# All blocks of the first two modulations asked for at once, with other loads moved behind them

## The chip, the cores and the metric

The kernel runs on one core of a Trainium2 chip. The metric is the device time of one execution in microseconds (us), as the median of several runs. Five engines work side by side, each through its own instructions in order: TensorE (PE in the profile, its weight loads PEld), VectorE (DVE), ScalarE (ACT), GpSimd (POOL) and SyncE (SP). SP computes nothing here; its queue holds nearly all requests for data, and each request goes to DMA engines that copy between HBM and SBUF while the engines work on. A few requests stand in ACT's queue, among its arithmetic.

## The reference

Two layers of a diffusion backbone over 256 latent and 256 context tokens of width 1024. Each layer is a SwiGLU half-step, a token mixer and a second half-step, all of them modulated by vectors that are computed from a conditioning vector with a large matrix `ada_w`:

```
mx = split(silu(c) @ ada_w[i] + ada_b[i], 9)       # latent; mh: the same from c_ctx, for the context
h  = modulate(rms_norm(x, g), shift, scale)         # h * (1 + scale) + shift
x  = x + 0.5 * gate * ((silu(h @ w_gate) * (h @ w_up)) @ w_down)     # half-step, inner width 2816
xn, hn = modulated norms of latent and context; ox, oh = mixer(xn, hn)
x  = x + mx[5] * ox;   then the second half-step, for the latent and (in layer 0) the context
```

The first half-step of a stream needs three of the nine modulation vectors: shift (0), scale (1) and gate (2). Everything is float32.

## The kernel before

**Tiles.** Activations are kept transposed, as 8 tiles of 128 features x 256 tokens per stream. Weights come in blocks of 128 x 1024 (512 KB). A float32 product is made of three matmuls: ACT rounds a half-block to `whi` (line 224), DVE computes the rest `wlo` (line 227), and PE multiplies `hh` by `whi`, `hl` by `whi` and `hh` by `wlo`, 8 such triples for one block.

**The front.** `ada_first` computes shift and scale, in 8 steps `t` of 128 features. Each step asks for two half-blocks of 512 KB (`raw<-in_ada_first`, line 218), multiplies them on PE (8 matmuls, `f` or `aux` `<-raw,scpad`), has ACT copy the sums (`sqa`, line 337), adds on PE (`<-selq,sqa`) and ends with two small operations on DVE (`mod`, lines 340 and 341). With those two `norm_h` makes one of the eight tiles `hh`, `hl` (lines 461, 462 and 467). `abreast` multiplies each tile, as soon as it is there, with the gate and up weights of blocks 0 and 1 of the inner width; these four weight blocks sit in a pool of their own (`front`). When `abreast` has been written out, a callback `done` closes that pool.

**The first half-step of the context** (`ffn00c`). The inner width has 22 blocks of 128. Blocks 2, 3, ... each take two products (a gate and an up block, `f<-hh,whi` and so on), then `gated` (lines 512, 513) and a split (255, 256) whose results are kept in `rows` tiles `ah`, `al`. The blocks are in groups, (0, 8), (8, 15) and (15, 22): after each group `down` multiplies its results with the down weights, 8 products, and adds them to x (`residual`, line 472). Room for weight blocks on the way: 5 tiles `raw`.

**Beside the products.** `next(beside)` runs one step of other modulation work after each block and after every second product of `down`: first 16 steps of `ada_rows` (one block of 512 KB and two products on DVE of 128 x 1024 each, `junk`, line 371; modulations 2 and 3), then steps of `more_ada` (two blocks of 512 KB, 4 or 8 matmuls `aux`). `ada_rows` needs `srow`, 1 MB that `ada_vectors` asks for and sends through Silu on ACT (lines 358, 360). The gate has to be complete before the first `down`, so `ffn` takes further steps there if need be.

**Order.** Each engine runs its instructions in the order of a scheduler that works on the order in which the code is written; generators stand side by side in `weave`, each with a rank and a clock, and `yield "rows"` makes one wait for the mark of that name. All requests share 8 completion slots in turn: a request waits until the request eight before it has landed, on whichever queue that was.

Of the kernel before, what the change touches and what calls it, by code (L numbers as in the profile page):

```python
# [21 lines left out]
NF = 22  # L22
# [1802 lines left out]
class Main(Net):  # L1825
    def run(self):
        self.tc.cur_priority -= 2000
        self.setup()
        self.tc.cur_priority += 2000
        with ExitStack() as self.m0s:  # L1830
            Mixer0.shared(self, self.m0s, "left")
            self.spawn(self.contexts(), 0)
            self.spawn(self.latents(), 0)
            self.weave()

    def contexts(self):

        st, fx, first = ExitStack(), ExitStack(), []
        front = self.pool(fx, "front", "left")

        def begin():
            def after(t):
                if t < 2:
                    first.extend(self.fetch(front, self.I["ffn_gu"][0, 2 * t + e], 4) for e in range(2))
            self.load_x(0)
            with ExitStack() as raw:
                self.ada_first(self.pool(raw, "raw", "left"), 8, after)

        def beside(*at):
            self.ada_vectors(self.pool(st, "st", "left"))  # L1850
            yield from self.steps(self.ada_rows(range(2, 4)), *at)
            st.close()
            self.mark("rows")
            yield from self.more_ada(*at)
        self.ffn(0, 0, 0, "right", "ffn00c", 50, begin=begin, raws=5, bufs=4, rows=8, extra=beside, groups=((0, 8), (8, 15), (15, NF)),
                 front=(front, first), done=fx.close)
        yield "ffn00c"
        self.m0c = Mixer0(self, 0, "right", 10)
        self.m0c.chain(10, None)
        yield "endm00"  # L1860
        self.ffn(0, 1, 0, "right", "ffn01c", 60.5, raws=4, bufs=4, rows=6, tanh=True, extra=self.more_ada)
        yield "ffn10c"
        self.m1.context("right", 30)

    def latents(self):

        yield 20.0
        self.load_x(1)
        Mixer0.consts(self)
        yield "rows"  # L1870
        self.ffn(0, 0, 1, "left", "ffn00x", 60, raws=4, bufs=4, rows=6, tanh=True, extra=self.more_ada)
        yield "ffn00x"
        m0x = Mixer0(self, 1, "left", 20)
# [4 lines left out]
        with ExitStack() as st:  # L1878
            self.ada_vectors(self.pool(st, "st", "left"))
            early, rows = self.ada_rows(range(10, 12)), self.ada_rows(range(12, 18))  # L1880
# [30 lines left out]
```

## Time and profile before

| | us |
|---|---|
| time, median of 3 runs | 2132.99 (2126.71 to 2137.01) |
| the profiled execution, its own time | 2136.58 |
| span of the profiled execution | 2134.7 |
| PE busy | 2041.3 (96%) |
| DVE, ACT busy | 1442.4 (68%), 992.2 (46%) |
| DMA | 361 MB, mean 169 GB/s |
| mean granted clock of PE | 0.976 |

The profiled execution is 3.6 us above the median. All places below are given in us from the start of the span. Three places are used as marks: at 53.43 the front's last modulated tile reaches PE, at 153.8 the 16 steps of `ada_rows` are complete, and at 294.4 the last residual of the first half-step of the context ends.

### The profile page before, as it was taken

Reading aid. Unit: us, or ns where it says so; the run is one execution under the profiler, and the core shown is the slowest. Engines: PE = TensorE matmul, PEld = TensorE weight load, DVE = VectorE, ACT = ScalarE, POOL = GpSimd, SP = SyncE. Lnnn points to the kernel's source line nnn. Section 1 sums busy time; section 2 is a strip of 40 time slices with the busy share of each in tenths; the row PEclk is TensorE's granted clock in tenths of the full one; section 3 lists DMA queues with packets and bytes.
Section 4 is the critical chain, followed back from the end, with each engine's and each line's share of the span. In section 5 each row is a group of like instructions: output and inputs, shape, how many; then the busy total and the mean of one; then the engine's idle time right before and its main releaser. Section 6 shows DMA issues by size and latency. Waiting matters only on the chain.

```text
span 2134.7 us, 41784 instructions
## 1 busy us (share of the span) xinstructions
PE 2041.3 (96%) x16120; PEld 1855.8 (87%) x16120; DVE 1442.4 (68%) x3193; ACT 992.2 (46%) x2084; POOL 195.0 (9%) x364
## 2 busy tenths in 40 slices
PE   6999899999999989999998999999999999998999
PEld 4897778899889889988998999988878987888999
DVE  4794467896567889855678966884654485656554
ACT  3443346554435665534455445432232457435553
POOL 0000006601000194010100000000000010000000
PEclk9899999999999999989999999999999999999999
DMA  8678765555244436622356665674554342224554
GB/s 324 203 259 305 252 236 193 154 181 155 80 136 158 140 119 188 172 87 81 127 192 205 217 229 150 212 232 156 209 168 143 91 134 87 75 86 147 184 178 120
DMA packets 131492, 361.04 MB, mean 169 GB/s; under 512 B 30652, under 2 KB 39612, under 8 KB 131037
## 3 DMA queue, kind: packets, MB, share of 16 engines
q1 hardware_dynamic: 129808, 356.58, 51.0%
q8 instruction: 126, 2.06, 0.4%
q10 hardware_dynamic: 1484, 1.80, 0.3%
q14 instruction: 74, 0.60, 0.1%
HBM read 352.82 MB, written 5.51 MB: 168 GB/s over the span
## 4 chain that ended last, share of the span: by engine, by line
PE 75%; DMA 9%; DVE 8%; ACT 3%; issue 3%; POOL 1%; SPq 0%; DVEq 0%; ACTq 0%; POOLq 0%
PE f L175 45%; PE mm L175 19%; PE g L175 6%; DVE wlo L227 3%; DMA raw<-in_ffn_gu 3%; DMA raw<-in_ada_rows 3%; DMA raw<-in_ffn_down 2%; PE q L175 1%; PE aux L175 1%; ACT whi L224 1%; DVE junk L371 1%; PE mm L185 1%; DVE hn L461 1%; DMA srow<-in_c_rows 1%; DVE x L472 0%
## 5 line engine op out<-in xcount | busy, mean ns | idle before, releaser
L224 ACT CAST whi<-raw 128x512 fp32r<-128x512 f32 (+3 forms) x1082 | 625.8, 594 | 760.7 <-PE f L175 378.0
L227 DVE TENSOR_TENSOR wlo<-raw,whi 128x512 fp32r<-128x512 f32 (+3 forms) x1082 | 709.9, 670 | 339.6 <-ACT whi L224 320.8
L175 PE MATMUL f<-hh,whi 128*128 128x256 f32 x1696 | 487.8, 288 | 9.8 <-ACT whi L224 5.1
L175 PE MATMUL f<-hh,wlo 128*128 128x256 f32 x1696 | 487.6, 288 | 5.4 <-DVE wlo L227 5.3
L175 PE MATMUL f<-hl,whi 128*128 128x256 f32 x1696 | 486.7, 287 | 1.8 <-DVE hl L467 1.7
L175 PEld LDWEIGHTS f<-hh,whi 128*128 128x128 f32 x1696 | 328.5, 194 | 23.5 <-ACT whi L224 12.5
L175 PEld LDWEIGHTS f<-hh,wlo 128*128 128x128 f32 x1696 | 328.4, 194 | 13.5 <-DVE wlo L227 9.6
L175 PEld LDWEIGHTS f<-hl,whi 128*128 128x128 f32 x1696 | 328.8, 194 | 4.0 <-DVE hl L467 3.0
L175 PE MATMUL f<-ah,whi 128*128 128x256 f32 (+1 forms) x1040 | 309.9, 298 | 12.2 <-ACT whi L224 6.9
L175 PE MATMUL f<-ah,wlo 128*128 128x256 f32 (+1 forms) x1040 | 308.7, 298 | 5.8 <-DVE wlo L227 5.6
L175 PE MATMUL f<-al,whi 128*128 128x256 f32 (+1 forms) x1040 | 307.5, 296 | 0.1
L175 PEld LDWEIGHTS f<-ah,whi 128*128 128x128 f32 x1040 | 204.1, 196 | 26.2 <-ACT whi L224 13.6
L175 PEld LDWEIGHTS f<-ah,wlo 128*128 128x128 f32 x1040 | 203.9, 196 | 13.3 <-DVE wlo L227 9.3
L175 PEld LDWEIGHTS f<-al,whi 128*128 128x128 f32 x1040 | 204.3, 196 | 3.9 <-issue 0.5
L371 DVE SCALAR_TENSOR_TENSOR junk<-raw,srow 128x1024 int8<-128x1024 f32 x128 | 156.6, 1223 | 75.1 <-DMA raw<-in_ada_rows 72.9
L175 PE MATMUL mm<-whi,hh 128*128 128x256 f32 x368 | 101.2, 294 | 4.9 <-ACT zk L1548 2.8
L175 PE MATMUL mm<-wlo,hh 128*128 128x256 f32 x368 | 104.8, 291 | 1.1 <-DVE wlo L227 0.9
L175 PE MATMUL mm<-whi,hl 128*128 128x256 f32 x368 | 102.3, 287 | 1.0 <-DVE hl L467 1.0
L255 ACT CAST ah<-sg 128x256 fp32r<-128x256 f32 (+1 forms) x134 | 58.3, 435 | 93.0 <-DVE sg L513 78.8
L472 DVE SCALAR_TENSOR_TENSOR x<-f,mod,x 128x256 f32<-128x256 f32 x144 | 63.5, 479 | 34.3 <-PE f L175 33.6
L175 PEld LDWEIGHTS mm<-whi,hh 128*128 128x128 f32 x368 | 67.8, 192 | 10.1 <-ACT zk L1548 3.8
L175 PEld LDWEIGHTS mm<-wlo,hh 128*128 128x128 f32 x368 | 70.9, 193 | 6.3 <-issue 3.1
(480 smaller groups left out, 3538.5 us busy)
## 6 DMA issues: line engine op xcount, KB each, us to landing
raw<-in_ffn_gu SPq DMA_DIRECT2D x268, 512.0 KB, 4.3
raw<-in_ada_rows SPq DMA_DIRECT2D x80, 512.0 KB, 4.3
raw<-in_ffn_down SPq DMA_DIRECT2D x56, 512.0 KB, 3.9
raw<-in_ada SPq DMA_DIRECT2D x48, 512.0 KB, 5.8
raw<-in_ffn_down SPq DMA_DIRECT2D x56, 384.0 KB, 3.2
raw<-in_ev_qkv SPq DMA_DIRECT2D x24, 512.0 KB, 3.8
raw<-in_ev_nat SPq DMA_DIRECT2D x20, 512.0 KB, 4.2
raw<-in_ffn_down SPq DMA_DIRECT2D x32, 320.0 KB, 3.0
```

Source lines behind the costliest of these rows:

```text
L175: self.nc.tensor.matmul(out, lhsT=lhsT, rhs=rhs, start=start, stop=stop, **kw)
L185: self.nc.tensor.transpose(out, src, self.c["ident"][:n, :n])
L224: self.nc.scalar.copy(hi[:, :w], raw[:, :w])
L227: (self.nc.gpsimd if self.cut % P == P - 1 else self.nc.vector).tensor_tensor(lo[:, :w], raw[:, :w], hi[:, :w], op=ALU.subtract)
L255: self.nc.scalar.copy(pair[0], src)
L371: nc.vector.scalar_tensor_tensor(self.junk, raw, 1.0, self.srow[:, s], op0=ALU.mult, op1=ALU.mult, accum_out=self.mod[:, m, t, s:s + 1])
L461: nc.vector.scalar_tensor_tensor(hn, self.x[s][k], scale, r, op0=ALU.mult, op1=ALU.mult)
L472: self.nc.vector.scalar_tensor_tensor(self.x[s][k], pb, self.mod[:, gate, k, s:s + 1], self.x[s][k], op0=ALU.mult, op1=ALU.add)
```

## The change

- `ada_first` gets room for 16 half-blocks rather than 8: all that it ever asks for.
- `Mixer0.shared`, which reserves the first mixer's room (and the pool for its constants), is called in `done`, so that `ada_first`'s blocks can lie where that room is later.
- `ada_vectors` (the 1 MB `srow`) moves from the start of `beside` into `done`.
- `latents` waits for the mark "rows" before it loads the latent stream x1 and the mixer's constants (`Mixer0.consts`: `const` 611 KB, `ev_rows` 112 KB, `ev_conv` 30 KB, `ev_cols` 5 KB, requested on ACT's queue), rather than for 20.0 on the clock of `weave`.
- The groups of the first half-step become (0, 9), (9, 16) and (16, 22), with 9 `rows` tiles.

```diff
         with ExitStack() as self.m0s:
-            Mixer0.shared(self, self.m0s, "left")
             self.spawn(self.contexts(), 0)
             self.spawn(self.latents(), 0)
             self.weave()
...
             self.load_x(0)
             with ExitStack() as raw:
-                self.ada_first(self.pool(raw, "raw", "left"), 8, after)
+                self.ada_first(self.pool(raw, "raw", "left"), 16, after)
+
+        def done():
+            fx.close()
+            Mixer0.shared(self, self.m0s, "left")
+            self.ada_vectors(self.pool(st, "st", "left"))
 
         def beside(*at):
-            self.ada_vectors(self.pool(st, "st", "left"))
             yield from self.steps(self.ada_rows(range(2, 4)), *at)
             st.close()
             self.mark("rows")
             yield from self.more_ada(*at)
-        self.ffn(0, 0, 0, "right", "ffn00c", 50, begin=begin, raws=5, bufs=4, rows=8, extra=beside, groups=((0, 8), (8, 15), (15, NF)),
-                 front=(front, first), done=fx.close)
+        self.ffn(0, 0, 0, "right", "ffn00c", 50, begin=begin, raws=5, bufs=4, rows=9, extra=beside, groups=((0, 9), (9, 16), (16, NF)),
+                 front=(front, first), done=done)
...
     def latents(self):
 
-        yield 20.0
+        yield "rows"
         self.load_x(1)
         Mixer0.consts(self)
-        yield "rows"
         self.ffn(0, 0, 1, "left", "ffn00x", 60, raws=4, bufs=4, rows=6, tanh=True, extra=self.more_ada)
```

A block of 9 k-tiles of down weights is wider than one `raw` tile, so `product` asks for it as 128 x 1024 and 128 x 128 (64 KB), each in a tile of its own.

What SP asks for in a row, from the tenth request of the front on; x_3 is the latent stream x1, raw a block of weights. Before:

```order
L218 DMA raw_219<-in_ada_first 128x1024
L286 DMA x_3_67<-in_xT 128x1024 x2
L218 DMA raw_221<-in_ada_first 128x1024
L218 DMA raw_536<-in_ffn_gu 128x1024
L218 DMA raw_580<-in_ffn_gu 128x1024
L218 DMA raw_622<-in_ada_rows 128x1024
L218 DMA raw_629<-in_ffn_gu 128x1024
L218 DMA raw_668<-in_ffn_gu 128x1024
L218 DMA raw_238<-in_ada_first 128x1024
```

Five more `ada_first` and `srow` follow. Now, from the same place:

```order
L218 DMA raw_256<-in_ada_first 128x1024
L218 DMA raw_258<-in_ada_first 128x1024
L218 DMA raw_513<-in_ffn_gu 128x1024
L218 DMA raw_557<-in_ffn_gu 128x1024
L218 DMA raw_591<-in_ada_rows 128x1024
L218 DMA raw_598<-in_ffn_gu 128x1024
L218 DMA raw_637<-in_ffn_gu 128x1024
L286 DMA x_3_67<-in_xT 128x1024 x2
L358 DMA srow_501<-in_c_rows 128x2048
L218 DMA raw_671<-in_ada_rows 128x1024
```

The two rows at the head are the last of the 16 blocks; seven blocks that stood ahead of the last six of them (two of x1, four of ffn_gu, one of ada_rows) stand behind now.

ACT near the end of the front, now (before, the four requests stand at the very start of its queue). hh is a modulated tile, sqa the copy of a step's sums, const and the ev_ tiles the first mixer's constants:

```order
L462 ACTIVATE hh_76_323<-hn_322,mod_79 128x256
L292 DMA const_390_1882<-in_const 128x1222
L296 DMA ev_conv_1884<-in_ev_conv 128x60
L296 DMA ev_rows_1886<-in_ev_rows 128x224
L337 COPY sqa_250<-aux_241 128x256
L296 DMA ev_cols_1888<-in_ev_cols 128x10
L462 ACTIVATE hh_79_329<-hn_328,mod_79 128x256
L337 COPY sqa_269<-f_260 128x256
```

The four requests stand ahead of the copies of the last two steps; by the slots in turn they wait for the landing of the last `ada_first` block, of the next two `ffn_gu` blocks and of the `ada_rows` block.

DVE at the end of the front, before: mod is the modulation of one step (L340, L341) or of a row (L371).

```order
L467 SCALAR_TENSOR_TENSOR hl_108_387<-hn_385,mod_79,hh_107_386 128x256
L371 SCALAR_TENSOR_TENSOR junk_618,mod_79<-raw_622,srow_617 128x1024 x2
L340 TENSOR_SCALAR mod_79<-f_280,adab_72 128x2
L341 TENSOR_SCALAR mod_79<-f_280,b_36_133,ng_74 128x2
L461 SCALAR_TENSOR_TENSOR hn_391<-x_2_66,mod_79,q_296 128x256
```

Now the front runs through to its last tile, and the first products with `srow` come 21 instructions after that; the place where they stand now (acc is the sum of squares of x1):

```order
L434 TENSOR_TENSOR acc_5_69<-acc_5_69,sq_386_1872 128x256
L227 TENSOR_TENSOR wlo_656<-raw_637,whi_655 128x512
L513 TENSOR_TENSOR sg_151_632<-sg_151_632,f_510 128x256
L434 TENSOR_TENSOR acc_5_69<-acc_5_69,sq_387_1875 128x256
L256 TENSOR_TENSOR al_512<-sg_151_632,ah_511 128x256
L371 SCALAR_TENSOR_TENSOR junk_502,mod_79<-raw_591,srow_501 128x1024 x2
L227 TENSOR_TENSOR wlo_681<-raw_678,whi_680 128x512
```

What moved: the first two of the 32 products with `srow` from ahead of the last `mod` of the front to behind blocks 2 and 3, and five sums of x1 into that stretch.

## Rows read from the trace of the kernel before

**Rows 1.** The profile's page: PE in 40 slices of 53.4 us; the longest chain.

```profile
PE   6999899999999989999998999999999999998999
PE 75%; DMA 9%; DVE 8%; ACT 3%; issue 3%; POOL 1%; SPq 0%; DVEq 0%; ACTq 0%; POOLq 0%
```

**Rows 2.** Stretches: length, busy time of five engines, PE clock, DMA share, GB/s.

```profile
10.00:46.00 36.00, 30.34 (x227) 19.68 (x227) 16.49 (x50) 12.63 (x29) 0.00 (x0) 0.95 1.02 407
46.00:53.00 7.00, 3.97 (x36) 3.23 (x34) 4.48 (x11) 2.90 (x5) 0.00 (x0) 0.89 0.06 15
53.00:69.00 16.00, 14.45 (x67) 14.16 (x68) 8.46 (x19) 5.85 (x12) 0.00 (x0) 0.51 0.50 157
69.00:92.00 23.00, 23.00 (x194) 23.00 (x193) 20.80 (x44) 11.99 (x25) 0.00 (x0) 1.00 0.60 204
92.00:106.00 14.00, 10.95 (x84) 10.13 (x83) 11.93 (x24) 4.99 (x11) 0.00 (x0) 1.00 0.75 243
106.00:154.00 48.00, 48.00 (x383) 47.03 (x383) 45.06 (x83) 21.09 (x38) 0.00 (x0) 0.96 0.80 261
154.00:294.00 140.00, 127.52 (x940) 104.20 (x941) 66.86 (x138) 54.16 (x110) 0.00 (x0) 0.98 0.76 267
```

**Rows 3.** SP's queue in the front: start, length of the issuing, what.

```profile
17.55 1.61 SPq L286 DMA_DIRECT2D x<-in_xT  x2
...
23.95 0.33 SPq L218 DMA_DIRECT2D raw<-in_ada_rows  x1
25.22 1.62 SPq L218 DMA_DIRECT2D raw<-in_ffn_gu  x2
27.85 8.17 SPq L218 DMA_DIRECT2D raw<-in_ada_first  x6
36.98 0.33 SPq L358 DMA_DIRECT2D srow<-in_c_rows  x1
```

**Rows 4.** Waits of SP's queue, 0 to 120: total, times, longest.

```profile
SPq L218 <- DMA raw<-in_ada_first: 11.1, 9, 3.0
```

**Rows 5.** Timeline, end of the front: start, length, engine, what, [idle before].

```profile
46.19 0.64 PE L175 MATMUL f<-raw,scpad 128*32 128x256 f32 x8
...
49.42 1.23 DVE L371 SCALAR_TENSOR_TENSOR junk<-raw,srow 128x1024 int8<-128x1024 f32 x1 [1.60 <-ACT srow L360]
...
50.77 1.23 DVE L371 SCALAR_TENSOR_TENSOR junk<-raw,srow 128x1024 int8<-128x1024 f32 x1
...
53.43 0.58 PE L175 MATMUL g<-hh,whi 128*128 128x256 f32 x1 [3.46 <-ACT hh L462]
```

**Rows 6.** Timeline of DVE: the last row product, and the half-step's last residual.

```profile
152.58 1.22 DVE L371 SCALAR_TENSOR_TENSOR junk<-raw,srow 128x1024 int8<-128x1024 f32 x1
...
293.88 0.48 DVE L472 SCALAR_TENSOR_TENSOR x<-f,mod,x 128x256 f32<-128x256 f32 x1 [3.09 <-PE f L175]
```

**Rows 7.** DMA issues: count, KB each, median us from issue to landing.

```profile
srow<-in_c_rows SPq DMA_DIRECT2D x1, 1024.0 KB, 11.3
const<-in_const ACTq DMA_DIRECT2D x1, 611.0 KB, 8.2
```

**Rows 8.** DMA issues of the whole run, small ones: the same columns.

```profile
kc<-mTk SPq DMA_DIRECT2D x8, 96.0 KB, 2.1
...
zg<-zt SPq DMA_DIRECT2D x4, 32.0 KB, 3.7
```

**Rows 9.** The chain that ended last, inside the first half-step: start, length, what.

```profile
191.06 1.07 PE aux L175 x8
...
231.69 5.48 DMA raw<-in_ffn_gu
...
239.66 6.54 DMA raw<-in_ffn_gu
```

**Rows 10.** Groups of DVE, 50 to 160: count, busy us, mean ns of one.

```profile
L227 DVE TENSOR_TENSOR wlo<-raw,whi 128x512 fp32r<-128x512 f32 x63 | 42.3, 688 | 11.2 <-ACT whi L224 11.1
L371 DVE SCALAR_TENSOR_TENSOR junk<-raw,srow 128x1024 int8<-128x1024 f32 x32 | 39.1, 1221 | 4.8 <-DMA raw<-in_ada_rows 3.1 <-ACT srow L360 1.6
```

## The prediction

> **What bounds the kernel now.** I first read the page: PE is busy in nine tenths or more of nearly every slice of 53 us, and the longest chain lies on PE for 75% [rows 1]. A change at the start is worth something only where PE waits or runs slowly, and the first slice is such a place: six tenths. So I went to stretches [rows 2]. The reader is to see four regimes there. From 10 to 46 the DMA engines are full (share 1.02, 407 GB/s), and PE, busy 30.3 of 36, works on what lands. From 46 to 53 the DMA engines stand idle and PE too; then, from 53 to 69, PE's granted clock is 0.51, its lower level of 1.2 GHz, after a stretch in which it was busy 4.0 of 7. From 69 to 154 DVE is the fullest engine (77.8 us busy of 85), though PE is busy nearly all the time as well. From 154 on DMA and PE share the bound: 127.5 of 140 us of PE, while 267 GB/s arrive.
>
> Then the timeline at the end of the front [rows 5]. The matmuls of the last `ada_first` block start at 46.19, but its tile reaches PE only at 53.43. Between them DVE has worked off two row products, at 49.42 and 50.77, which stand ahead of the last `mod` in its queue and waited for `srow` (released by ACT's Silu on it). SP's queue tells why that block is so late [rows 3]: the last six `ada_first` blocks are asked for from 27.85 to 36, behind x1, four `ffn_gu` blocks (one pair stands in the rows, from 25.22) and one `ada_rows` block.
>
> The profiled execution took 2136.58, 3.6 more than the median of the runs shown; the sum is made against it, and the 3.6 are taken off at the end.
>
> **The change, part by part.**
>
> *The front.* Seven blocks move behind the last `ada_first` block: 7 x 524 KB at 407 GB/s [rows 2] = 9.0 us. The mixer's constants (758 KB, `const` the largest [rows 7]) move behind it too: 1.9 us. So the last block lands 10.9 earlier, and its matmuls start at 35.3 rather than 46.19. From there to the last tile on PE it took 7.2 us, of which the two row products are 2 x 1.3 = 2.6; without them 39.9. Two things come later than that.
>
> ACT: the four requests for constants now stand ahead of the copies of the last two steps, and wait for blocks that land behind the last `ada_first` block: two `ffn_gu` (2.6 us later) ahead of the copy of step 6, one `ada_rows` (3.9) ahead of that of step 7. So the last copy is at 39.2 at the earliest; with copy, sums, `mod`, `hn` and `hh` behind it, each about half a microsecond and in turns over three engines, some 3.3 us, the last tile comes at 42.5.
>
> PE: until 53 it was busy for 30.3 + 4.0 = 34.3 us from about 10.5 on [rows 2]. The clock row of that stretch is 0.95 and 0.89, so some 1.5 of it is the lower level; PE can't be there before 10.5 + 32.8 = 43.3. I take **43.5** (42 to 48) in place of 53.43: a gain of 10 at this point, and PE rather than DMA bounds the front.
>
> The rate is a point on which the Trainium skill speaks. The row says 407 GB/s over 36 us. The page "DMA: Bandwidth & Descriptors", section "Specifications", gives 358 GB/s as what one core gets from HBM; the trace does not agree with it here, so the measurement decides. By the page's figure the same bytes would be worth 12.4 rather than 10.9, an estimate that changes nothing as PE is later than both.
>
> *The stretch to the last row product.* Before, it ended at 153.8 [rows 6]. From 53 to 154 DVE was busy 8.5 + 20.8 + 11.9 + 45.1 = 86.3 us and idle 14.7: 7.5 up to 69 and 7.2 after [rows 2]. The change adds to DVE behind the front: the two row products, 2.6; the five sums of x1 at the price of a 128x256 operation (0.48 [rows 6]), 2.4; one more block before the rows are complete (the ninth of the first group), four `wlo` at 0.69 [rows 10] and two small ones, 3.7; eight `wlo` of 128x128 for the tails. These have no row; 128x512 takes 0.69 and 128x256 0.48, and I continue the line to 0.37, so 3.0 (between nothing and 3.8). Sum 86.3 + 11.7 = 98.0. As to the idle time: in 53 to 69 a matmul took 14.45/67 = 0.216 us against 23.0/194 = 0.119 behind it, 6.5 us more for the 67, and DVE waited for them. The gap ahead of that stretch goes (PE now runs on to the last tile), so I take the clock to hold and 5 of the 7.5 to go. Of the other 7.2 I let 4.5 stand, since a fuller DVE fills some. So idle 7 (4.5 to 14.7): the rows are complete at 43.5 + 98 + 7 = **148.5**, gain 5.3 (from -2 to 9). Half of what the front gains is given back to DVE, which has more to do in less time.
>
> The cover for `srow` is thin: it is asked for behind x1, in memory that PE must first be done with, so at about 40; it took 11.3 to land [rows 7], and Silu takes a microsecond per half. It is ready at 52 to 53, and DVE needs it at about 43.5 + 2.5 + 10 = 56. If late, each us costs one.
>
> *One step fewer.* Behind the first `down` stood 18 steps of `more_ada` in the first half-step, now 17, because one more block has been done beside the rows. From 154 to 294 that is 140.5/18 = 7.8 us each, and the chain shows the same pace: from 231.69 to 239.66 one step, waiting for a block each time [rows 9]. Gain **7.8**. The bytes do not vanish: the step is made in the latent half-step, with two blocks and eight matmuls. It costs between those matmuls, 1.1 [rows 9], and the full 7.8. PE is busy in nine tenths there [rows 1], so I take the price of PE's work, a little over the low end: **-1.5**.
>
> *The groups.* The last group is 6 wide instead of 7: eight blocks of down weights are 64 KB smaller, 0.5 MB at 267 GB/s = 2.0 us if DMA bounds alone; I take **+1** (0 to 2). The first group is 9 wide, and pays with eight tails of 64 KB. Their bytes and their products are the ones taken elsewhere, but each takes a tile of its own of the five, an issue on SP and a landing. Issued two ahead they are hidden behind the products (8 triples of matmuls, 2.9 us at 0.119). I take nothing for that; the bounds are zero and eight landings of the nearest small transfers, 2.1 to 3.7 us [rows 8].
>
> A rule of the Trainium skill speaks against these tails: the page "DMA: Bandwidth & Descriptors", section "Anatomy of one DMA", puts a fixed 2.0 us on every transfer, and the section "Bandwidth" calls those under 64 KB descriptor-dominated. By the estimate from that page, 2.15 us each, none hidden, the eight would cost 17 us and the change would bring nothing; no tail is in this trace.
>
> *Order elsewhere.* Requests and instructions of both mixers stand in a slightly other order; all the work is the same. PE is busy in nine tenths or more there [rows 1]. I take zero, with 5 on either side.
>
> **Sum:** 5.3 + 7.8 - 1.5 + 1 = 12.6. 2136.6 - 12.6 = 2124.0, and 3.6 less for the median: 2120.4, so **2120**.
>
> **The rivals.**
>
> 1. *The gain is taken back behind the front.* PE's clock falls again (what precedes it is the same mix of `ada_first` and `abreast`, with waits on ACT), or `srow` comes late. For: it fell before at just this place. Against: the idle 46 to 53 was made by the row products. Price: the 5 us of idle come back, gain 12.6 - 5 = 7.6: 2125.
> 2. *The change does not do what it says.* All blocks have room, but only eight transfers are under way: SP already waited nine times for an `ada_first` landing, 11.1 in all [rows 4], and the ACT requests hold the copies. For: those slots are in the order of the requests. Against: with the DMA engines full the waits cost nothing. If the last tile comes at 50, DVE's row products end at 155 less what its idle time then absorbs, about 152; gain 1.8 + 7.8 - 0.5 = 9: 2124.
> 3. *Slower: the tails.* Every product of the first `down` waits for its tail, since five tiles are full and the request is issued only when one comes free. For: from 92 to 106, where this `down` begins, PE lost 3 of 14 us [rows 2]. Against: DVE, not DMA, is the fullest there. Each product then costs a landing of 2.1 to 3.7 [rows 8]. The gain is gone from 12.6/8 = 1.6 us on, and it is slower by half a per cent from (12.6 + 10.7)/8 = 2.9 on; at 3.2 each 25.6, so 13 slower: 2146.
> 4. *More than forecast.* DVE's idle time falls to 2 and the moved step is free: gain 20, 2112.
>
> **How the numbers follow.** Half a per cent (10.7 us) is about what a measurement of this kernel can tell from no change: faster is below 2122.3, slower above 2143.7. Forecast 0.55, rival 1 0.17, rival 2 0.09, rival 3 0.09, rival 4 0.10. The forecast's own spread, by the bounds of 43.5, of the idle time and of the mixers, is about 8 either side, so 0.39 of its 0.55 is faster by over half a per cent; with rival 4 and a little of 1 and 2 that makes 0.54. Slower 0.07, the rest 0.39. The range leaves out the outer part of rival 4 and rival 3: 2106 to 2133.
>
> **What would show it.** Timeline: the last `ada_first` matmuls at 35 to 37, the last tile on PE at 42 to 48, no row product before it. Stretches: a PE clock near 1.0 behind the front (rival 1: near 0.5 for more than 10 us). DVE: the last row product at 145 to 152 (rival 2: later). The chain from 92 on: `ffn_down` landings of 64 KB one per product would be rival 3. The end of the half-step at about 281; what it gains there and has no more at the span's end went into the latent half-step or the mixers. I am wrong if the front is early but the row products end at 153 or later, or if a moved request makes an engine wait in the mixers, where nothing here was costed.

## The result and the profile after

The changed kernel took 2108.89 us, median of four runs (2103.58 to 2113.63); the kernel before 2132.67 beside it. The ratio is 0.9896, with an interval from 0.9868 to 0.9924. A second comparison of the same two, with six runs of the changed kernel, gave 2110.47 and 0.9911 (0.9881 to 0.9941). So it is faster by 22 to 24 us, a little over one per cent; the forecast was 12.6 (2120, range 2106 to 2133). The execution profiled first, 2103.58, is the fastest of its four, so what its trace shows is about 5 us on the good side, while the trace of before lies 4 us on the other.

The stretches of the changed kernel, with the columns of [rows 2]:

```profile
10.00:46.00 36.00, 35.16 (x269) 25.03 (x266) 17.35 (x51) 12.28 (x26) 0.00 (x0) 1.00 1.02 404
46.00:53.00 7.00, 6.78 (x57) 6.60 (x56) 6.98 (x17) 6.46 (x18) 0.00 (x0) 1.00 0.58 172
53.00:69.00 16.00, 16.00 (x137) 16.00 (x136) 14.81 (x32) 9.43 (x20) 0.00 (x0) 1.00 0.73 237
69.00:92.00 23.00, 22.92 (x189) 22.47 (x187) 20.84 (x46) 11.53 (x25) 0.00 (x0) 1.00 0.69 229
92.00:106.00 14.00, 10.77 (x76) 10.40 (x75) 12.38 (x25) 3.28 (x7) 0.00 (x0) 0.88 0.68 196
106.00:154.00 48.00, 46.36 (x366) 43.41 (x366) 43.81 (x87) 24.44 (x50) 0.00 (x0) 1.00 0.88 295
154.00:294.00 140.00, 134.36 (x961) 103.89 (x960) 67.15 (x147) 53.22 (x109) 0.00 (x0) 1.00 0.75 261
```

The reader is to see three things against [rows 2]. The hole from 46 to 53 is gone, and PE's clock is 1.00 from 10 to 92. From 53 to 69 PE made 137 matmuls instead of 67. And in the last stretch PE is busy 134.4 of 140 instead of 127.5.

The end of the front, from the changed kernel's timelines (start, length, what, and in brackets the idle time before). SP's queue:

```profile
8.85 14.44 SPq L218 DMA_DIRECT2D raw<-in_ada_first  x12
...
41.02 0.33 SPq L358 DMA_DIRECT2D srow<-in_c_rows  x1
```

ACT and its queue:

```profile
34.52 0.34 ACTq L292 DMA_DIRECT2D const<-in_const  x1
...
37.51 0.38 ACT L337 COPY sqa<-aux 128x256 f32<-128x256 f32 x1 [2.61 <-PE aux L175]
38.36 0.34 ACTq L296 DMA_DIRECT2D ev_cols<-in_ev_cols  x1
38.74 0.51 ACT L462 ACTIVATE hh<-hn,mod 128x256 fp32r<-128x256 f32 x1 [0.86 <-DMA raw<-in_ada_rows]
```

PE, the last `ada_first` block and the last tile:

```profile
39.91 0.64 PE L175 MATMUL f<-raw,scpad 128*32 128x256 f32 x8
...
44.06 0.39 PE L175 MATMUL g<-hh,whi 128*128 128x256 f32 x1
```

DVE, the first and the last row product:

```profile
55.23 1.23 DVE L371 SCALAR_TENSOR_TENSOR junk<-raw,srow 128x1024 int8<-128x1024 f32 x1 [0.54 <-ACT srow L360]
...
143.12 1.22 DVE L371 SCALAR_TENSOR_TENSOR junk<-raw,srow 128x1024 int8<-128x1024 f32 x1
```

All 16 `ada_first` blocks are asked for by 23.3. The last block's matmuls start at 39.91 (before 46.19, [rows 5]), and the last tile reaches PE at 44.06 (before 53.43). The first row product starts at 55.23, after waiting 0.54 for Silu: the thin cover of `srow` was just used up. The rows are complete at 144.4 (before 153.8), and the last residual of the first half-step ends at 274.1 (before 294.4).

Fourteen executions were profiled. The table cuts each at three places: the rows complete; the last residual of the first half-step; and the residual (line 472) that ends at 1065 in the kernel before, behind which all kernels do the same in nearly the same order. The middle part holds the half-step of the latent, the first mixer and the second half-steps. The rest runs to the last residual of all, 3.0 before the span's end. All in us; the median is that of all runs of the kernel in its comparison. The first trace of the kernel with one empty step is of an execution of 2099.85, 12 below that kernel's median.

| kernel | rows complete | to half-step end | middle | rest | median |
|---|---|---|---|---|---|
| before | 153.8 | 140.6 | 771.0 | 1066.3 | 2132.7 |
| before, again | 153.4 | 140.7 | 771.1 | 1065.1 | 2131.4 |
| before, one empty step | 147.1 | 131.1 | 756.2 | 1060.6 | 2111.9 |
| the same, again | 152.3 | 131.5 | 762.5 | 1064.7 | 2110.4 |
| changed | 144.4 | 129.7 | 760.6 | 1064.1 | 2108.9 |
| changed, again | 146.4 | 131.4 | 764.3 | 1068.0 | 2110.5 |
| changed, old groups | 140.1 | 135.2 | 769.7 | 1066.0 | 2116.0 |
| changed, old groups, one empty step | 143.4 | 130.7 | 761.4 | 1063.7 | 2105.1 |
| the same, x1 early | 142.7 | 130.7 | 761.2 | 1065.1 | 2103.8 |
| changed, x1 early | 146.5 | 128.2 | 763.8 | 1064.0 | 2106.5 |
| changed, 8 rooms | 158.7 | 129.6 | 762.3 | 1065.8 | 2118.0 |
| changed, tails doubled | 151.1 | 131.9 | 758.6 | 1062.4 | 2108.9 |
| changed, two empty steps | 146.8 | 126.4 | 761.2 | 1065.9 | 2106.1 |
| changed, constants on SP | 145.8 | 130.1 | 763.1 | 1066.2 | 2110.6 |

The change's gain in the two traces of each kernel is thus some 8 us up to the rows, 10 from there to the half-step's end, and 7 to 10 in the middle, which the prediction had priced at a loss of 1.5 with 5 either way.

### The profile page after: what moved, and what is told of

Same layout as the page of the kernel before. It is cut to its first block, busy times and chain, and to the rows that moved or that the text cites. A ratio compares the mean times of both kernels' runs of the same rounds, so it can differ in the third digit from the quotient of the medians.

```text
span 2101.8 us, 41808 instructions
## 1 busy us (share of the span) xinstructions
PE 2022.7 (96%) x16120; PEld 1835.2 (87%) x16120; DVE 1439.8 (69%) x3201; ACT 990.5 (47%) x2092; POOL 196.5 (9%) x364
## 4 chain that ended last, share of the span: by engine, by line
PE 75%; DMA 8%; DVE 7%; POOL 3%; issue 3%; ACT 3%; SPq 0%; DVEq 0%; ACTq 0%; POOLq 0%
PE f L175 46%; PE mm L175 17%; PE g L175 6%; DMA raw<-in_ada_rows 4%; DVE wlo L227 3%; PE aux L175 2%; DMA raw<-in_ffn_gu 2%; DVE junk L371 1%; PE q L175 1%; POOL tap L872 1%; PE mm L185 1%; ACT whi L224 1%; DMA raw<-in_ffn_down 1%; DVE x L472 1%; DMA raw<-in_ev_nat 0%
## 5 line engine op out<-in xcount | busy, mean ns | idle before, releaser
L224 ACT CAST whi<-raw 128x512 fp32r<-128x512 f32 (+2 forms) x1090 | 626.3, 591 | 731.8 <-PE f L175 362.1
L227 DVE TENSOR_TENSOR wlo<-raw,whi 128x512 fp32r<-128x512 f32 (+2 forms) x1090 | 706.9, 662 | 322.2 <-ACT whi L224 301.5
L371 DVE SCALAR_TENSOR_TENSOR junk<-raw,srow 128x1024 int8<-128x1024 f32 x128 | 156.4, 1222 | 75.3 <-DMA raw<-in_ada_rows 74.2
L175 PE MATMUL mm<-whi,hl 128*128 128x256 f32 x368 | 101.5, 285 | 0.3 <-DVE hl L467 0.3
```

Source lines behind the costliest of these rows:

```text
L175: self.nc.tensor.matmul(out, lhsT=lhsT, rhs=rhs, start=start, stop=stop, **kw)
L224: self.nc.scalar.copy(hi[:, :w], raw[:, :w])
L227: (self.nc.gpsimd if self.cut % P == P - 1 else self.nc.vector).tensor_tensor(lo[:, :w], raw[:, :w], hi[:, :w], op=ALU.subtract)
L371: nc.vector.scalar_tensor_tensor(self.junk, raw, 1.0, self.srow[:, s], op0=ALU.mult, op1=ALU.mult, accum_out=self.mod[:, m, t, s:s + 1])
```

## The experiments

**The kernel before, once more.**

> The kernel before once more, nothing changed, for a second trace. Theory (the order in the mixers is worth nothing; what the two profiles differ by behind the first half-step of the latent is PE's clock, which falls at other places in every execution): time 2127 to 2137, ratio 1.00 within 0.004; the front's last tile reaches PE at 53 to 54, the rows are complete at 152 to 156, the first half-step ends at 291 to 297; between there and the end of the first mixer the second trace differs from the first by up to 8 us, and low-clock stretches stand at other places. Rival (the new order in the mixers is worth the 10 us by which the two profiles drift apart from 294 to 1041): the residuals of this trace stand where those of the first trace of before stand, within 2 us, all the way.

Nothing is edited. Ratio 1.0009 (0.9990 to 1.0027). The rival was right: up to 1065 the residuals stand where those of the first trace stand, within 1 us but for a few in the context's half-step, and behind that within 4.4; the long falls of PE's clock begin at the same places (51, 386, 703 and 908 us), some of the short ones do not. The profile of before can be read as typical, and what a changed kernel gains in the middle part is no luck of this one trace.

**The old groups in the changed kernel.**

> The changed kernel with the groups of before, (0, 8), (8, 15), (15, 22), and 8 rows tiles; the rest as changed. Theory (one step of more_ada costs 7.6 to 7.8 in the first half-step and 1 to 3 in the latent one; tails cost next to nothing): the last tile still at 44, the rows complete one block earlier in the count and at 141 to 146, the first half-step ends at 281 to 285 rather than 274.1, time 4 to 8 above the changed kernel's, 2113 to 2117. Rival (the tails cost about as much as the step saves): the half-step ends within 2 us of 274, time within 2 of the changed kernel's.

```diff
-rows=9, extra=beside, groups=((0, 9), (9, 16), (16, NF)),
+rows=8, extra=beside, groups=((0, 8), (8, 15), (15, NF)),
```

2116.0, ratio 0.9933 (0.9911 to 0.9955). The half-step ends at 275.3, only 1.2 later than with the new groups, where 7 to 11 were expected: the ninth block and the tails put the rows off by 4.3 in this pair of traces (144.4 against 140.1; two later kernels with the old groups have 142.7 and 143.4, so it may be as little as 1), and the step fewer then wins 5.5 (135.2 against 129.7). But the middle takes 769.7, as in the kernel before, and not 760.6. So most of what the new groups are worth comes behind the half-step, where neither theory had looked.

This run shows a second thing. From the rows to the half-step's end it takes 135.2 us, though it has the steps and the groups of the kernel before, which takes 140.6. With the columns of [rows 2]:

```profile
140.10:275.30 135.20, 128.22 (x946) 104.27 (x945) 66.89 (x139) 53.74 (x110) 0.00 (x0) 0.97 0.79 279
```

PE's work is that of the kernel before (128.2 against 128.1) and its idle time 7.0 instead of 12.5. So some 5 us of what the changed kernel gains in this stretch come without the moved step. What brings them is not shown, and it is one trace.

**Room for eight blocks.**

> The changed kernel with room for 8 blocks of ada_first instead of 16; the rest as changed. In the queue x1, four ffn_gu and one ada_rows stand ahead of the last seven ada_first again, but no row product stands ahead of the last modulation. Theory (the front of before was late by the seven blocks and by the two row products, and each can be taken back apart): the last ada_first block's matmuls start at 45 to 48, the last tile reaches PE at 49 to 52, the rows are complete at 149 to 153, time 2112 to 2118. Rival (PE or ACT bounds the front, the blocks' order is worth little): last tile at 44 to 46, time within 2 of the changed kernel's.

```diff
-self.ada_first(self.pool(raw, "raw", "left"), 16, after)
+self.ada_first(self.pool(raw, "raw", "left"), 8, after)
```

2118.0, ratio 0.9939 (0.9919 to 0.9960). The front is later than expected, later even than before: the last tile is at 54.70, though no row product stands ahead of it, and the rows are complete at 158.7. ACT's timeline shows what was not expected:

```profile
34.77 0.34 ACTq L292 DMA_DIRECT2D const<-in_const  x1
36.05 0.33 ACTq L296 DMA_DIRECT2D ev_conv<-in_ev_conv  x1
37.33 0.33 ACTq L296 DMA_DIRECT2D ev_rows<-in_ev_rows  x1
38.61 0.33 ACTq L296 DMA_DIRECT2D ev_cols<-in_ev_cols  x1
38.99 0.42 ACT L428 ACTIVATE acc<-x 128x256 f32<-128x256 f32 x1 [5.99 <-DMA raw<-in_ada_first]
```

The four requests for constants hold ACT for 6.0 us, because each waits for the landing of the block eight requests before it, and the copies of four steps stand behind them; PE then waits 5.46 us for the first of these copies, until 40.93. With 16 rooms the same requests stand later among ACT's copies and cost nothing that can be seen. The kernel is nevertheless 13 us faster than before, with a front that is 1.3 later. So more than half of the change's gain needs no earlier front.

**x1 early.**

> The changed kernel with x1 requested as in before (20.0 on the clock), the constants as changed; in the queue x1 stands right behind the last ada_first block, ahead of the four ffn_gu. Theory (the front is bounded by PE, its loads have all been asked for ahead of x1): last tile at 43 to 46, block 2 starts up to 2.6 later on its weights, rows complete within 2 us of 144.4, time within 3 of the changed kernel's, 2106 to 2113. Rival (where x1 stands is worth as much as two blocks, 2.6, on each thing behind it): the rows are complete at 147, time 2111 to 2114.

```diff
-        yield "rows"
+        yield 20.0
         self.load_x(1)
+        yield "rows"
         Mixer0.consts(self)
-        yield "rows"
```

2106.5, ratio 0.9890 (0.9869 to 0.9911): within 3 us of the changed kernel. The last tile is at 44.55. Where x1 stands behind the front is worth nothing that can be measured.

**One empty step in the kernel before.** The runs so far point to the step that moves and to the order that comes of it. In `beside`, the generator gives control back once without doing anything, so every later step of `more_ada` comes one place later. The front and its loads stay as they were; behind the first `down` of the latent half-step the order of the matmuls is nearly word for word that of the changed kernel; between there and the end of the context's half-step the two differ. The requests show the moved step: up to the end of the context's half-step 36 blocks of `raw<-in_ada` are asked for, as in the changed kernel, and 38 in the kernel before.

> The kernel before with one empty step behind the rows, so that one step of more_ada moves from the first half-step into the latent one, and nothing else: no other room, loads or groups. Its matmuls in the latent half-step and the first mixer then stand in the order of the changed kernel. Theory (the moved step is worth 5 to 8 in the first half-step, costs 2 to 3 in the latent one, and the order that follows from it is worth 5 in the first mixer): front and rows as before (53, 153 to 154), the half-step ends at 286 to 289, time 2119 to 2125. Rival (what the changed kernel gains in the mixer is luck of PE's clock, or comes from the early front): half-step end as in the theory, but nothing behind it, time 2125 to 2129.

```diff
             self.mark("rows")
+            yield
             yield from self.more_ada(*at)
```

2111.9, ratio 0.9908 (0.9873 to 0.9943): 18.6 less than the kernel before in its comparison. This is more than the theory had for it, and nearly what the whole change brings. It was run again:

> The kernel before with the one empty step, once more: how much of the change's gain the moved step and its order have by themselves. Theory (the rows complete at 147 in the first trace because the clock fell for 3 us rather than 17 behind the front, which other executions do not share; the step and the order come back): the stretch from the last row product to the half-step end 130 to 133 again, the first mixer as before less 5, time 2109 to 2117, that is 14 to 21 below the kernel before. Rival (its median was luck): time 2119 to 2125.

2110.4, ratio 0.9910 (0.9880 to 0.9940), in the same comparison in which the changed kernel had 2110.5. From the rows to the half-step's end it takes 131.1 and 131.5 us instead of 140.6: 9 us, not 7.8, for one step. The stretches of the kernel before, with the columns of [rows 2]:

```profile
153.80:294.40 140.60, 128.12 (x945) 104.40 (x943) 67.26 (x141) 54.16 (x110) 0.00 (x0) 0.98 0.76 266
294.40:1065.00 770.60, 750.62 (x7170) 692.81 (x7167) 570.21 (x1373) 399.29 (x913) 175.59 (x291) 0.97 0.46 144
```

And of this one, in its second trace:

```profile
152.30:283.80 131.50, 125.39 (x922) 99.55 (x921) 66.43 (x137) 50.95 (x105) 0.00 (x0) 1.00 0.79 274
283.80:1046.30 762.50, 745.23 (x7186) 692.48 (x7181) 568.69 (x1374) 400.98 (x915) 175.00 (x292) 0.97 0.47 147
```

Of the 9 us, 2.7 are PE's work and 6.4 its idle time (12.5 before, 6.1 now): PE waits for loads at the step's pace, and with one step less there is less to wait for. In the middle, the step that came in adds work, and still the part takes 8 us less.

**The step without the ninth block.**

> The changed kernel with the groups and rows tiles of before and one empty step behind the rows: the moved step without the ninth block and without tails. Theory (the step is what the wider group is worth; its block and its tails cost 4): rows complete at 140 to 141, half-step end at 268 to 271, first mixer in the order of the changed kernel, time 2103 to 2109, at or below the changed kernel. Rival (the wider group is worth its gain by itself, by down products of 9): half-step end at 274 or later, time 2110 to 2116.

The edit is the two above together: the old groups and the empty step, in the changed kernel. 2105.1, ratio 0.9888 (0.9843 to 0.9932). The time is as expected, the places are not: the rows are complete at 143.4, not 140 to 141 (the last tile came at 45.87 here, 2.0 later than with the old groups alone), and the half-step ends at 274.1 as in the changed kernel, not at 268 to 271. Against the old groups alone the stretch from the rows to the half-step's end falls from 135.2 to 130.7 and the middle from 769.7 to 761.4. So the gain of the new groups is that of the step. The ninth block and the tails are not needed for it; whether they cost something is not settled by the times (2105.1 against 2108.9 and 2110.5, with overlapping intervals).

**The tails doubled.**

> The changed kernel with the number of tails doubled: the down weights of the first group are asked for as 7, 1 and 1 k-tiles instead of 8 and 1, so 16 transfers of 64 KB, each in a raw tile, instead of 8. Theory (a tail is hidden behind the products): rows complete 1 to 3 later than 144.4 by eight more small operations on DVE and ACT, half-step end within 3 of 274.1, time 2108 to 2112. Rival (each tail costs its landing, 2 to 3.5): rows complete 16 or more later, time above 2120.

```diff
-        for a in range(0, n, 8):
-            b = min(n, a + 8)
+        for a, b in ((0, 7), (7, 8), (8, 9)) if n == 9 else [(a, min(n, a + 8)) for a in range(0, n, 8)]:
```

2108.9, ratio 0.9908 (0.9873 to 0.9944). The tails among the DMA issues from 80 to 125 (count, KB, median us to landing) in the changed kernel:

```profile
raw<-in_ffn_down SPq DMA_DIRECT2D x8, 64.0 KB, 3.5
```

And with the tails doubled:

```profile
raw<-in_ffn_down SPq DMA_DIRECT2D x16, 64.0 KB, 2.7
```

Each takes 2.7 to 3.5 us to land. Eight more put the rows off to 151.1, 5.7 behind the mean of the changed kernel's two traces (144.4, 146.4): 0.7 us each, between the theory's and the rival's. It is not the small operations that cost this. From 44 to the rows, in the second trace of the changed kernel (the stretch with the columns of [rows 2], then the row products):

```profile
44.00:146.40 102.40, 97.01 (x777) 94.79 (x776) 92.11 (x188) 50.85 (x106) 0.00 (x0) 0.98 0.73 242
L371 DVE SCALAR_TENSOR_TENSOR junk<-raw,srow 128x1024 int8<-128x1024 f32 x32 | 39.1, 1221 | 1.6 <-DMA raw<-in_ada_rows 0.9 <-ACT srow L360 0.5
```

And with the tails doubled:

```profile
44.00:151.10 107.10, 97.28 (x757) 94.09 (x757) 92.86 (x195) 50.70 (x112) 0.00 (x0) 0.97 0.69 230
L371 DVE SCALAR_TENSOR_TENSOR junk<-raw,srow 128x1024 int8<-128x1024 f32 x32 | 39.0, 1219 | 5.0 <-DMA raw<-in_ada_rows 4.3 <-ACT srow L360 0.5
```

DVE is busy only 0.8 us longer, and idle 14.2 instead of 10.3; the row products wait 4.3 instead of 0.9 us for their `ada_rows` blocks, which stand behind the added tails in SP's queue. The time is not longer; in this one trace the middle gave 2 to 6 us back, for no reason that was looked into.

**Two empty steps.**

> The changed kernel with two empty steps behind the rows, so that two more steps of more_ada move into the latent half-step. Theory (each moved step saves 5 to 8 while DMA bounds, less as PE becomes the bound): half-step end at 261 to 268, 4 to 8 given back in the latent half-step; order of both mixers new, worth between -5 and 5: time 2100 to 2112. Rival (the first half-step is bounded by PE by now): end at 270 or later, time 2108 to 2116.

2106.1, ratio 0.9900 (0.9866 to 0.9934). The half-step ends at 273.1, not at 261 to 268, so the rival was right. From the rows to there it takes 126.4, 3 to 5 us less than the changed kernel. But these are not the price of two steps: up to the half-step's end 34 blocks of `raw<-in_ada` are asked for, one step fewer than the changed kernel's 36, and as many matmuls of the steps (128) run there, since what is executed on which side of that mark is not fixed by the code alone. PE is near its bound, busy 123.1 of 126.3. In total nothing that can be told from the changed kernel.

**The changed kernel, once more.**

> The changed kernel once more, for a second trace and a firmer median. Theory (its half-step end and its first mixer belong to the order and come back; what differs from execution to execution is where PE's clock falls and for how long): last tile at 44, rows complete at 143 to 147, half-step end at 273 to 277, first mixer as in the first trace within 2 us, time 2105 to 2112, ratio to the kernel before 0.987 to 0.992. Rival (the first trace was a lucky one throughout): half-step end above 278, time above 2113.

The ratio is given above. Last tile (44.94) and rows are within 2 us of the first trace, the half-step ends at 277.8, a little behind the 273 to 277 expected, and the middle takes 764.3; the times reach from 2105.7 to 2114.8, and the profiled execution is the slowest of them. The theory holds otherwise, and the first trace was a good one.

**The constants on SP's queue.**

> The changed kernel with the first mixer's constants requested on SP's queue instead of ACT's, so that they stand behind x1 and ahead of srow, and nothing holds ACT's copies in the front. Theory (PE bounds the front, so ACT's waits are worth 1 us at most; srow comes a little later by 1.9 us of constants): last tile at 43 to 44.5, first row product at 55 to 58, half-step end within 3 of 274.1, time 2105 to 2113. Rival (ACT's waits hold the front): last tile at 41 or earlier, time below 2105.

```diff
-        self.nc.scalar.dma_start(out=cb, in_=self.I[f"const{which}"])
+        (self.nc.sync if which == 1 else self.nc.scalar).dma_start(out=cb, in_=self.I[f"const{which}"])
```

(and the three small ones likewise.) 2110.6, ratio 0.9910 (0.9880 to 0.9940). ACT's copies of the last two steps are then at 38.33 and 41.63, each after waiting for PE (2.47 and 2.49), and no earlier than in the changed kernel (37.51 and 40.67). The last tile is at 45.03. ACT's requests do not hold the changed kernel's front; PE does.

**The parts that are worth something, together.**

> The changed kernel with the groups of before, the empty step behind the rows, and x1 asked for at 20.0 on the clock as in before: the front's 16 rooms and the moved step, without the ninth block, its tails, and the late x1. Theory (the two parts that are worth something, put together without those that cost): last tile at 43 to 46, rows complete at 140 to 144, half-step end at 270 to 274, time 2101 to 2107. Rival (no better than the changed kernel): time 2107 to 2112.

The changed kernel with the old groups, the empty step and x1 early. All places and the time are as expected: 2103.8 (2094.2 to 2105.6), ratio 0.9868 (0.9834 to 0.9902), against 0.9911 (0.9881 to 0.9941) for the changed kernel in the same comparison. Its median is the lowest of all, 6.7 below the changed kernel's; the intervals overlap, so it is likely but not certain that it beats it.

## Why the prediction was right, and where not

**The front: right.** 43.5 was forecast for the last tile, and it came at 44.06. The bound was the one named, PE: it was busy 35.2 of 36 us from 10 to 46. The matmuls of the last block start at 39.91 and not at 35.3, since they stand in PE's queue behind work that the sum had not placed there; this cost nothing. ACT's requests and their waits were there as the order said (the copy at 37.51 stands behind three of them), and were covered. The Trainium skill's figure of 358 GB/s (page "DMA: Bandwidth & Descriptors", section "Specifications", which has it as the rate of a stack of HBM divided by two cores) is passed again: 404 GB/s over 36 us, with this kernel on one core.

**The rows: the right sign, 148.5 forecast, 144.4 and 146.4 measured.** The term that was mis-sized is DVE's work. The first two stretches of the changed kernel (first trace), with the columns of [rows 2]:

```profile
44.00:69.00 25.00, 24.75 (x204) 24.40 (x204) 22.61 (x49) 16.89 (x38) 0.00 (x0) 1.00 0.69 226
69.00:144.40 75.40, 70.45 (x559) 68.62 (x558) 69.08 (x139) 33.01 (x68) 0.00 (x0) 0.98 0.78 253
```

DVE was busy 22.6 + 69.1 = 91.7 us, not 98.0, and idle 8.7, not 7. Its groups from 44 to 144.4 (count, busy, mean ns of one):

```profile
L227 DVE TENSOR_TENSOR wlo<-raw,whi 128x512 fp32r<-128x512 f32 x62 | 41.3, 687 | 6.3 <-ACT whi L224 4.8 <-PE f L175 1.1
...
L227 DVE TENSOR_TENSOR wlo<-raw,whi 128x128 fp32r<-128x128 f32 x8 | 2.3, 288 | 0.0
L434 DVE TENSOR_TENSOR acc<-acc,sq 128x256 f32<-128x256 f32 x5 | 2.1, 418 | 0.0
```

The tails and the sums are there at 2.3 and 2.1 (forecast 3.0 and 2.4). But there are 62 `wlo` of the large size, where the kernel before has 60 between its own two marks: of the ninth block's four only two lie ahead of the last row product. The sum had counted a whole block, with two small operations that are not there either (11 `al` and as many `sg` in both kernels). By these groups the additions come to 7.7 us, not 11.7; the other 2.3 of the 6.3 are not accounted for.

The prediction had DVE take back half of what the front gains. It did not: from the last tile to the rows the stretch takes 100.4 us in the kernel before and 100.3 and 101.5 in the changed kernel's two traces.

**PE's clock behind the front: taken to hold, and it held; but the row it was read from was not what it seemed.** The sum let 5 us of DVE's idle time go because the hole ahead of the stretch goes. In the changed kernel the clock was 1.00 there. Yet the kernel with one empty step has the front of before, hole and all, and its first trace has this (with the columns of [rows 2]):

```profile
52.00:56.00 4.00, 2.69 (x13) 2.69 (x14) 1.51 (x5) 2.04 (x5) 0.00 (x0) 0.70 0.43 133
56.00:60.00 4.00, 2.99 (x24) 2.70 (x24) 4.00 (x8) 2.30 (x5) 0.00 (x0) 0.88 0.23 53
60.00:64.00 4.00, 4.00 (x35) 4.00 (x35) 3.49 (x11) 1.62 (x3) 0.00 (x0) 1.00 0.82 279
64.00:68.00 4.00, 4.00 (x36) 4.00 (x35) 3.02 (x8) 1.55 (x4) 0.00 (x0) 1.00 0.54 197
```

and the second trace of the kernel before, at the same instructions:

```profile
52.00:56.00 4.00, 2.69 (x12) 2.69 (x13) 1.61 (x5) 1.92 (x4) 0.00 (x0) 0.50 0.41 133
56.00:60.00 4.00, 3.22 (x16) 2.93 (x15) 4.00 (x9) 1.99 (x6) 0.00 (x0) 0.50 0.26 75
60.00:64.00 4.00, 4.00 (x20) 4.00 (x20) 2.43 (x7) 0.84 (x2) 0.00 (x0) 0.50 0.76 265
64.00:68.00 4.00, 4.00 (x20) 4.00 (x20) 1.09 (x4) 0.70 (x2) 0.00 (x0) 0.50 0.31 102
```

The same hole is followed by a fall to 1.2 GHz of some 3 us in one execution and by one of 14 to 17 us in three; the rows are then complete at 147.1 or at 152.3 to 153.8. The changed kernel's 144.4 and 146.4 stand against the one or the other. With the short fall the stretch from the last tile to the rows took 93.8 us, so against that trace the changed kernel does take some 7 more, as DVE's added work would have it; the clock gives them back only against an execution with the long fall.

**One step fewer: the right stretch, and the size partly luck.** 7.8 was forecast, by the mean pace of the 18 steps, and the stretch from the rows to the half-step's end is 9 to 11 shorter. In the kernel before, the empty step by itself is worth 9.1 to 9.6 there. But in the changed kernel the step is worth 4 to 5.5 (135.2 with the old groups against 130.7 with the empty step, and 129.7 and 131.4 with the new groups); the other 5 came with the rest of the change, and no term of the sum had them.

**What failed: "order elsewhere, zero, with 5 on either side".** The moved step changes the order of nearly everything up to some 840 us, and that was priced at nothing. The same piece of the context's first mixer, beside which the latent half-step runs, with the columns of [rows 2], in the kernel before:

```profile
442.00:690.00 248.00, 248.00 (x2538) 231.05 (x2537) 173.80 (x410) 121.37 (x288) 17.43 (x49) 0.99 0.44 137
```

In the changed kernel with the old groups:

```profile
426.30:674.30 248.00, 248.00 (x2538) 231.05 (x2537) 173.82 (x410) 121.25 (x288) 17.43 (x49) 0.99 0.44 136
```

In the changed kernel:

```profile
423.70:666.70 243.00, 242.87 (x2535) 229.93 (x2534) 174.45 (x415) 120.58 (x282) 16.87 (x49) 0.99 0.46 142
```

In the kernel with the empty step, second trace:

```profile
428.90:671.90 243.00, 242.87 (x2523) 229.78 (x2522) 173.20 (x411) 119.10 (x275) 16.35 (x49) 0.98 0.45 140
```

The first two have one order and take 248.0; the last two have the other and are through in 243.0, the changed kernel with 3 matmuls fewer and the kernel with the empty step with 15 fewer. PE is busy all the time, and the clock is no higher. Between two residuals that all kernels have (the last of the first `down` of the latent half-step, and the last of that half-step) the stretch reads thus in the kernel before, the changed kernel and the kernel with the empty step (second trace):

```profile
431.40:701.40 270.00, 269.36 (x2715) 252.12 (x2713) 193.90 (x464) 132.96 (x314) 17.43 (x49) 0.99 0.45 141
413.20:678.00 264.80, 264.18 (x2712) 250.95 (x2710) 193.91 (x470) 133.74 (x315) 16.87 (x49) 0.99 0.46 142
416.60:683.50 266.90, 266.25 (x2717) 252.87 (x2715) 194.38 (x470) 133.12 (x314) 16.35 (x49) 0.98 0.45 140
```

The other traces of the three have 270.1, 264.8 and 267.0, and the changed kernel with the old groups 271.4. So the order is worth 5 us in the changed kernel and 3 with the empty step, where more of the stretch runs at the lower clock; every trace of one order is below every trace of the other. Why the one order is quicker is not shown. The rows of the small matmuls say only where some of the time lies; those of the kernel before from 442 to 690 (count, busy, mean ns):

```profile
L175 PE MATMUL g<-vn,w 64*64 64x64 f32 x128 | 8.8, 223 | 0.0
...
L175 PE MATMUL g<-S,qT 64*64 64x64 f32 x96 | 4.6, 226 | 0.0
```

And of the changed kernel from 423.7 to 666.7:

```profile
L175 PE MATMUL g<-vn,w 64*64 64x64 f32 x128 | 7.8, 221 | 0.0
...
L175 PE MATMUL g<-S,qT 64*64 64x64 f32 x96 | 3.2, 225 | 0.0
```

The rest of the middle part is partly PE's clock: between 890 and 930 it is 0.83 in the kernel before and 1.00 in the changed one, but 0.84 in the kernel with the empty step, so this share comes and goes. And from the end of the context's half-step to the last residual of the first `down` of the latent one the kernel with the empty step takes 132.1 and 132.8 us, the kernel before 137.0 and 137.6, the changed one 139.1 and 136.4. That is 4 to 5 us of what the empty step gains in the middle part, in part by the clock (1.00 against 0.97 and 0.98); in the changed kernel the stretch gains next to nothing. The step that moved in there was priced at 1.5, and no run shows that price by itself.

**The groups and the tails: the tails are mostly hidden, but not free.** The tails were taken as hidden but for their work on DVE. By the doubling one more costs 0.7 us at the rows, most of it in waits for `ada_rows` blocks that are asked for later, a term that the sum did not have; what the first eight cost is not shown by itself. The rule of the Trainium skill that speaks against them (a fixed 2.0 us for a transfer, page "DMA: Bandwidth & Descriptors", section "Anatomy of one DMA", there for transfers issued by GpSimd, while SP issues these) is borne out by the landings, 2.7 to 3.5 us, and not by the time: most of a landing passes while others are multiplied.

**The account.** Up to the rows 5.3 was forecast and 7 to 9 came, with the clock's share in it; from there to the half-step's end 8.8 (7.8 and 1) against 9 to 11; behind it a loss of 1.5 against a gain of 7 to 10. The step and its order bring 19 to 22 by themselves, nearly the whole gain, and the change without the step brings 15 (2116.0); together they bring 22 to 24, so the two do not add up, and the gain cannot be split between them. The front, which the prediction put first, gains 9.4 at the place where it is measured; in the time, the kernels with the early front, the step and the old groups (2105.1, 2103.8) are 5 to 8 below those with the step alone (2111.9, 2110.4), a difference about as large as the intervals. How much of the front is lost where was not settled. The rivals: the tails (3) did not come, nor did the second, and the first's long fall of the clock belongs to the front of the kernel before. The fourth named a time (2112; its own terms add up to 19 rather than 20, so 2114) that is nearer than the forecast's 2120, but not its road: DVE's idle time was 8.7 and not 2.

## What to carry to other kernels

Read what a change does to the interleaving of optional work, not only to the loads that it names: a step that moves from a stretch bounded by loads into one bounded by TensorE was worth 19 to 22 us here by itself, with the order that came of it, and one line did it; the earlier start without it was worth 15. The two do not add up here, so try each alone and both together. When an edit shifts such steps, all that follows is in another order and has a price of its own; several kernels that share the order, and one that has it without the rest of the change, show it at once. And where an edit moves requests to a queue that also computes, look for what stands behind them.

## What the runs showed of the hardware

- After the same idle stretch of PE, with the same instructions on either side, the granted clock stayed at its lower level for 14 to 17 us in three traces of four and for some 3 in one, though PE was fully busy in the second half of the long ones.
- Four requests on ACT's queue held its arithmetic for 6.0 us where the landings that they wait for were late, and PE behind it for 5.5.
- About 2,715 matmuls of the first mixer and the latent half-step took 264.8 to 267.0 us in one order (ten traces) and 270.0 to 271.4 in another (three), with PE busy all but some 0.7 us and the mean granted clock 0.98 to 1.00.
- Eight more transfers of 64 KB put the rows off by 4.7 and 6.7 us against two traces; DVE's own work was 0.8 of the 4.7, the rest waits, most of them for loads that stand behind those transfers in SP's queue.
